# An accumulating DMA in place of a subtraction, in the two stages that have tokens on the partitions

## The chip, the core and the metric

The kernel runs on one core of one Trainium2 chip. The time is device time of one execution, in microseconds. The kernel before takes 2176.35 us (median of two runs, 2176.28 and 2176.42).

A core has five engines with a queue of instructions each: TensorE (PE in the profile; PEld is its load of weights), VectorE (DVE), ScalarE (ACT), GpSimd (POOL) and SyncE (SP). Sixteen DMA engines move data between memory and the on-chip buffer, or inside that buffer. SP issues the loads here; they go out on a hardware queue. A DMA that POOL issues goes out on a software queue.

## What is computed

Two transformer blocks, one after the other, on 256 tokens of 2048 features, all in float32:

```
x = x + attention(rms_norm(x)) @ w_o                      # stick-breaking attention, 16 heads
x = x + relu(rms_norm(x) @ w1)**2 @ w2                    # 8192 hidden features
x = rms_norm(x)
m = concat(attention(z), pooling(z)) @ w_o_2              # z = rms_norm(x) @ w_in, 8 heads
x = x + rms_norm(m, post_mix_g)
up = causal_dwconv(rms_norm(x) @ w_up)                    # 2 x 5632 features
y = (gelu(up[:, :5632]) * up[:, 5632:]) @ w_down
x = x + rms_norm(y, post_ffn_g)
```

The two products behind which a norm of its own follows (`@ w_o_2` and `@ w_down`) are the two stages of the change.

## The kernel before

**Operands in two parts.** Every large product takes its operands in two parts: hi, the 12 leading bits (type float32r), and lo, the rest. Three of the four partial products are formed: hi x hi, hi x lo and lo x hi. The weights come from memory in float32 and are split on the chip.

**Units.** The weights are cut into about 400 units of at most 1024 KB (128 partitions x 2048 values). A unit is loaded into a tile raw (three of these), split into hi and lo by halves of 1024 columns (six tiles of each, so three units' worth), and multiplied. For each half, ScalarE writes hi (line 159: a copy of raw that rounds) and VectorE then writes lo = raw - hi (line 160).

**The order** is written out by hand at the end of `tile_two_blocks`. While unit i is multiplied, the load of unit i + 3 is issued on SP and the two halves of unit i + 2 are split; the part of a split that follows on another engine is emitted one place later (`rest`). Engines serve their instructions in the order in which they stand, each with its waits: a load waits until the raw tile's last reader is done, a split until PE is done with the unit whose hi and lo tiles it takes over.

**The two stages.** In most products the features are on the partitions. In the output projection of the second block (`w_o2`, 16 units of four blocks of K) and in the four passes over `w_down` (12 units each: 4 result chunks x units of 4, 4 and 3 blocks) the tokens are: hi and lo of the weights stream through PE as the moving operand (lines 218 to 220). Each w_down pass follows a fourth of the gated features (`w_up`, 22 units), whose last results, `ff`, it reads: POOL multiplies gate and value (line 908), ScalarE and VectorE split the result (lines 126 and 129).

Of the kernel before, what the change touches and what calls it, by code (L numbers as in the profile page):

```python
# [8 lines left out]
F32 = mybir.dt.float32  # L9
# [22 lines left out]

# Features are on the partitions and tokens along a row, but for the values of
# the attentions and for the two sums behind which a norm of its own follows:
# there the tokens are on the partitions.
#
# Every large product takes its operands in two parts, the 12 leading bits
# (float32r, exact in one pass) and the rest; three of the four partial
# products carry float32's accuracy.


class Unit:
    """One stretch of weights: its load, its split in two parts, its products."""

    def __init__(self, src, blocks, width, mm, evac):
        self.src = src
        self.blocks = blocks
        self.width = width
        self.mm = mm
        self.evac = evac  # L50
        self.acc = None
        self.halves = []

# [9 lines left out]
def tile_two_blocks(ctx: ExitStack, tc: tile.TileContext, xT, w_q_k, w_v, w_o, w1, w2,  # L63
# [48 lines left out]
    def later(n, fn):  # L112
        """Emit it n places on, when the other engines have what it needs."""
        if st.get("now"):
            fn()
        else:
            queue.setdefault(clock[0] + n, []).append(fn)

    def hold(first, n, step=None, place="A"):
        """The results of n units stay in PSUM until this step."""  # L120
        for k in range(first, first + n):
            late[k] = (first + n if step is None else step, place)

# [1 line left out]
    def hi_copy(dst, src, scale=1.0):  # L125
# [28 lines left out]
    def split(i, eng=V):  # L154
        """Two pieces of work, and what follows each of them a place later."""
        raw = units[i].raw
        for a, b, hi, lo in halves(i):
            hi, lo = hi[:, 0:b - a], lo[:, 0:b - a]
            A.activation(out=hi, in_=raw[:, a:b], func=AF.Copy)
            yield lambda a=a, b=b, hi=hi, lo=lo: eng.tensor_tensor(  # L160
                out=lo, in0=raw[:, a:b], in1=hi.bitcast(F32), op=ALU.subtract)

# [1 line left out]
    def block(u, j, op, first, last):  # L164
        """out[:, 0:T] + out[:, T:] gathers the three partial products."""
        hi, lo = u.w(j)
        if last:
            PE.matmul(u.acc[:, 0:T], lhsT=lo, rhs=op[:, 0:T], start=False, stop=False)  # L168
            PE.matmul(u.acc, lhsT=hi, rhs=op, start=False, stop=True)  # L169
        else:  # L170
            PE.matmul(u.acc, lhsT=hi, rhs=op, start=first, stop=False)  # L171
            PE.matmul(u.acc[:, 0:T], lhsT=lo, rhs=op[:, 0:T], start=False, stop=False)  # L172

    def features(u, ops, order=None, part=None):
        """Products with the features on the partitions: all of K, or a part of its order."""
        order = range(u.blocks) if order is None else order
        a, b = part or (0, len(order))
        if a == 0:
            u.acc = accum("acc")
        for n in range(a, b):  # L180
            block(u, order[n], ops[order[n]], n == 0, n == len(order) - 1)

    def pair(i, ops, order, tail, mid=None, end=None):
        """Two units at once: both take the operands that come last at the end."""
        u, v = units[i], units[i + 1]
        n = len(order)
        features(u, ops, order, (0, n - tail))
        if mid:
            mid()
        features(v, ops, order, (0, n - tail))  # L190
        features(u, ops, order, (n - tail, n))
        features(v, ops, order, (n - tail, n))
        if end:
            end()

    def keep_warm(n):
        """Products that nothing reads, where the tensor engine waits: its clock would halve."""
        ps = aux("ps_warm")
        for _ in range(n):
            PE.matmul(ps[:, 0:P], lhsT=ones, rhs=ones, start=True, stop=True)  # L200
# [4 lines left out]
    def tokens(some, accs, first, last, one_by_one):  # L205
        """Products with the tokens on the partitions, for a part of K."""
        wide = [slice(0, 512)]
        todo = [(n, k, t, c) for n, (u, _) in enumerate(some) for k in range(u.blocks)
                for t in range(2) for c in (HALVES if len(accs) > 2 and t else wide)]
        if one_by_one:  # L210
            todo.sort(key=lambda x: (x[2], x[3].start))
        for n, k, t, c in todo:
            u, ops = some[n]
            hi, lo = u.w(k)
            xh = ops[k][:, t * P:(t + 1) * P]
            xl = ops[k][:, T + t * P:T + (t + 1) * P]
            acc = accs[2][:, c] if c.start else accs[t][:, c]
            PE.matmul(acc, lhsT=xh, rhs=hi[:, c], start=first and n == k == 0, stop=False)  # L218
            PE.matmul(acc, lhsT=xh, rhs=lo[:, c], start=False, stop=False)  # L219
            PE.matmul(acc, lhsT=xl, rhs=hi[:, c], start=False,  # L220
                      stop=last and n == len(some) - 1 and k == u.blocks - 1)

    def token_units(srcs, ops, evac, apart=0):
        """The units of 512 result features: srcs has (weights, their tiles of K) of each.
        The last units (their number is apart) do one half of the tokens before the other."""
        accs = []
# [7 lines left out]
        for j, (src, nk) in enumerate(srcs):  # L234
# [9 lines left out]
            def ev(u, j=j):  # L244
                if j == n - 1:
                    evac(accs)
            units.append(Unit(src, nk, 512, mm, ev))
            at_k += nk

    def whole(u):  # L250
        """The second of the two sums, on its way to be added."""
        t = t256("half")
        A.activation(out=t, in_=u.acc[:, T:2 * T], func=AF.Copy)  # L253
        return t

# [1 line left out]
    class Stat:  # L257
# [21 lines left out]
    def root(src, dst):  # L279
        """(src / D + eps) ** -0.5, of a column or two."""  # L280
        n = src.shape[-1]
# [24 lines left out]

    # ================= the units =================
    xin = []
# [4 lines left out]

    # -- first block: q and k of each head, then v
    qk = {}
# [50 lines left out]
    def later_only(ap, fill):  # L366
        """A value where the key is not before the query: in the two diagonal blocks."""
        d = ap[:, 0:384].rearrange("p (b q) -> p b q", b=3)[:, 0:3:2, :]
# [85 lines left out]

    # -- output projection: the residual, and what feeds the MLP
    a2 = {}
# [40 lines left out]

    # -- MLP, a fourth of the hidden features at a time
    hid = {}
# [20 lines left out]
    def pairs(first, ops, n, tail, mid=None, end=None):  # L520
        """What the units of a new set of operands do: the first two go together."""
        def f(m):
# [20 lines left out]

    # -- second block
    B2 = len(units)
# [11 lines left out]

    # the residual turns its tokens onto the partitions
    resT = {}
# [85 lines left out]

    # -- pooling over trailing windows
    BU = len(units)
# [48 lines left out]

    # -- v, with the map of the pooled features between its chunks
    BV2 = len(units)
# [28 lines left out]
    class Ordered:  # L727
        """The operands of the output projection: first those that are there first."""
        def __getitem__(self, k):
            return o2[(k + 8) % 16]  # L730

    # -- output projection, with tokens on the partitions: a norm follows
    mg = {}
# [48 lines left out]
    for n in range(NC):  # L782
        token_units([(w_o2[n, j], 4) for j in range(4)], Ordered(), evac_o2(n), 1 if n == NC - 1 else 0)

    # -- gated feed-forward, a fourth of its features at a time
    BF = len(units)
# [178 lines left out]
    for fc in range(FC):  # L965
# [12 lines left out]
        for n in range(NC):  # L978
            w = w_down[fc, n]
            token_units([(w[:, a * 512:min(a + 4, FT) * 512], min(4, FT - a)) for a in range(0, FT, 4)],  # L980
                        ff, evac_down(fc, n), 2 if fc == FC - 1 and n == NC - 1 else 0)
    for n in range(4):
        hold(BF + n, 1, BF + 3 + n % 2, "C")

    # ================= the program =================
    gains = {}
# [101 lines left out]
def _blocks(w, kt, nt):  # L1088
    """(K, N) -> (N tiles, 128, K tiles, 128), each of them in one piece."""
    return w.reshape(kt, P, nt, P).transpose(2, 1, 0, 3)  # L1090


def _rows(w, kt, nc):
    """(K, N) -> (chunks of 512, fourths of K, 128, K tiles, 512)."""
    return w.reshape(4, kt // 4, P, nc, 512).transpose(3, 0, 2, 1, 4)
# [59 lines left out]
```

## Time and profile before

| | |
|---|---|
| median of the runs | 2176.35 us (2176.28 to 2176.42) |
| profiled execution, its span | 2174.6 us |
| PE busy | 2156.1 us, 99% |
| DVE, ACT, POOL busy | 1433.2, 1112.3, 201.3 us |
| moved by DMA | 401.13 MB, 184 GB/s over the span |

No time of its own is shown for the profiled execution but its span, from the first to the last instruction; it is 1.75 us under the median of the runs. Busy time says how much an engine did, not whether anyone waited for it: that is read from the chain of waits, and from the windows of the single stages. PE's ends are modelled, so 99% busy is not PE at its peak.

### The profile page before, as it was taken

To read this page: it belongs to the slowest core of one execution; us is meant where nothing else is said; L and a number is where in the kernel's file an instruction comes from. 1 tells how busy PE (TensorE), PEld (TensorE's weight loads), DVE (VectorE), ACT (ScalarE), POOL (GpSimd) and SP (SyncE) were. 2 spreads that over 40 slices of the span, in tenths; PEclk is the share of its full clock that TensorE was granted. 3 is DMA by queue.
4 is the path that set the end of the run, shared out by engine and by line. 5 is a ranking of instruction groups with operands and counts; after the bars stand their busy time and mean duration, and the time that the engine had idled before them with its cause. 6 is when DMAs were issued, how large, how long until landed. Compare 5 with 4: busy or idle time off the path is not lost.

```text
span 2174.6 us, 29627 instructions
## 1 busy us (share of the span) xinstructions
PE 2156.1 (99%) x11765; PEld 1858.6 (85%) x11765; DVE 1433.2 (66%) x2038; ACT 1112.3 (51%) x1682; POOL 201.3 (9%) x281
## 2 busy tenths in 40 slices
PE   8999999999999999999999999999999999999997
PEld 7888888888888888888888888888888888888886
DVE  8776546665565556556656665488758857866885
ACT  5555445454354355345546544466546545544653
POOL 4000001000000000000120150011101101100110
PEclk9999999999999999999999999999999999999999
DMA  7454545555555555555555555545555565555553
GB/s 256 157 173 173 177 162 187 176 192 194 177 192 192 178 190 178 191 186 182 194 175 193 179 184 192 203 143 186 202 194 184 180 200 192 178 190 194 189 204 111
DMA packets 60106, 401.13 MB, mean 184 GB/s; under 512 B 6848, under 2 KB 8000, under 8 KB 14144
## 3 DMA queue, kind: packets, MB, share of 16 engines
q1 hardware_dynamic: 59184, 397.13, 53.1%
q0 software_dynamic: 640, 2.10, 0.3%
q8 instruction: 93, 1.52, 0.3%
q14 instruction: 45, 0.37, 0.0%
q10 hardware_dynamic: 144, 0.01, 0.0%
HBM read 397.11 MB, written 2.10 MB: 184 GB/s over the span
## 4 chain that ended last, share of the span: by engine, by line
PE 98%; DVE 1%; issue 0%; ACT 0%; POOL 0%; DMA 0%; DVEq 0%; POOLq 0%
PE acc L171 46%; PE acc L172 23%; PE acc L218 7%; PE acc L220 7%; PE acc L219 7%; PE acc L169 3%; PE acc L168 2%; PE ps_o L436 0%; PE ps_z L362 0%; DVE xin L132 0%; DVE y L960 0%; PE ps_o L437 0%; PE ps_back L801 0%; PE ps_z L363 0%; PE ps_s L406 0%
## 5 line engine op out<-in xcount | busy, mean ns | idle before, releaser
L253 ACT ACTIVATE half<-acc 128x256 f32<-128x256 f32 x208 | 77.7, 377 | 215.9 <-PE acc L169 213.8
L462 DVE TENSOR_TENSOR res<-acc,res 128x256 f32<-128x256 f32 x80 | 33.9, 424 | 136.4 <-PE acc L169 136.4
L268 POOL TENSOR_TENSOR s<-s,sq 128x256 f32<-128x256 f32 x45 | 32.7, 741 | 861.1 <-ACT sq L267 861.1
L893 POOL TENSOR_TENSOR s<-s,c 128x256 f32<-128x256 f32 x44 | 36.1, 822 | 449.3 <-DVE s L892 449.3
L874 ACT ACTIVATE c<-half,vec 128x256 f32<-128x256 f32 x88 | 52.3, 595 | 35.6 <-DVE half L870 35.6
L511 ACT ACTIVATE sq_relu<-half 128x256 f32<-128x256 f32 x64 | 26.8, 419 | 71.3 <-DVE half L507 71.3
L881 DVE SCALAR_TENSOR_TENSOR c<-half,vec,c 128x254 f32<-128x254 f32 x88 | 58.0, 659 | 3.1
L897 ACT ACTIVATE s<-s 128x256 f32<-128x256 f32 x44 | 18.3, 418 | 71.0 <-POOL s L893 71.0
L126 ACT ACTIVATE ff<-c 128x256 fp32r<-128x256 f32 x44 | 18.4, 418 | 70.0 <-POOL c L908 69.9
L870 DVE TENSOR_TENSOR half<-half,rb 128x256 f32<-128x256 f32 x88 | 50.9, 578 | 3.1
L908 POOL TENSOR_TENSOR c<-gate,c 128x256 f32<-128x256 f32 x44 | 36.4, 827 | 146.1 <-DVE gate L902 138.7
L879 DVE SCALAR_TENSOR_TENSOR c<-half,vec,c 128x255 f32<-128x255 f32 x88 | 42.4, 482 | 0.0
L869 DVE TENSOR_TENSOR half<-acc,half 128x256 f32<-128x256 f32 x88 | 36.8, 418 | 0.0
L463 DVE TENSOR_TENSOR res<-acc,res 128x256 f32<-128x256 f32 x80 | 34.0, 425 | 2.7
L126 ACT ACTIVATE o<-ps_o 128x256 fp32r<-128x256 f32 x24 | 9.2, 384 | 50.9 <-PE ps_o L437 50.9
L506 DVE TENSOR_TENSOR half<-acc,half 128x256 f32<-128x256 f32 x64 | 26.8, 418 | 4.9 <-ACT half L253 4.9
L129 DVE TENSOR_TENSOR hid<-sq_relu,hid 128x256 fp32r<-128x256 f32 x64 | 26.8, 419 | 3.7 <-ACT hid L126 3.7
L507 DVE SCALAR_TENSOR_TENSOR half<-half,rb 128x256 f32<-128x256 f32 x64 | 27.2, 426 | 2.2
L126 ACT ACTIVATE a<-res,vec 128x256 fp32r<-128x256 f32 x16 | 8.1, 509 | 40.1 <-DVE res L463 40.1
L126 ACT ACTIVATE hid<-sq_relu 128x256 fp32r<-128x256 f32 x64 | 26.9, 420 | 2.0
L938 DVE TENSOR_TENSOR y<-acc,y 128x512 f32<-128x512 f32 x23 | 15.8, 692 | 16.8 <-PE acc L220 16.8
L392 ACT ACTIVATE sp_hi<-e 128x384 fp32r<-128x384 f32 x16 | 8.3, 524 | 35.5 <-POOL e L369 35.5
(6172 smaller groups left out, 8290.8 us busy)
## 6 DMA issues: line engine op xcount, KB each, us to landing
raw<-in_w SPq DMA_DIRECT2D x128, 1024.0 KB, 4.8
raw<-in_w_up SPq DMA_DIRECT2D x88, 1024.0 KB, 4.7
raw<-in_w_q_k SPq DMA_DIRECT2D x45, 1024.0 KB, 4.8
raw<-in_w_o SPq DMA_DIRECT2D x32, 1024.0 KB, 4.8
raw<-in_w_down SPq DMA_DIRECT2D x32, 1024.0 KB, 4.8
raw<-in_w_v SPq DMA_DIRECT2D x24, 1024.0 KB, 4.7
raw<-in_w_down SPq DMA_DIRECT2D x16, 768.0 KB, 4.1
raw<-in_w_u SPq DMA_DIRECT2D x8, 1024.0 KB, 4.8
```

The lines of the kernel that those rows point to most:

```text
L126: A.activation(out=dst[:, 0:T], in_=src, func=AF.Copy, scale=scale)
L168: PE.matmul(u.acc[:, 0:T], lhsT=lo, rhs=op[:, 0:T], start=False, stop=False)
L169: PE.matmul(u.acc, lhsT=hi, rhs=op, start=False, stop=True)
L171: PE.matmul(u.acc, lhsT=hi, rhs=op, start=first, stop=False)
L172: PE.matmul(u.acc[:, 0:T], lhsT=lo, rhs=op[:, 0:T], start=False, stop=False)
L218: PE.matmul(acc, lhsT=xh, rhs=hi[:, c], start=first and n == k == 0, stop=False)
L219: PE.matmul(acc, lhsT=xh, rhs=lo[:, c], start=False, stop=False)
L220: PE.matmul(acc, lhsT=xl, rhs=hi[:, c], start=False, stop=last and n == len(some) - 1 and k == u.blocks - 1)
L253: A.activation(out=t, in_=u.acc[:, T:2 * T], func=AF.Copy)
L870: V.tensor_tensor(out=t, in0=t, in1=st["rb6"], op=ALU.mult)
L874: A.activation(out=c, in_=t, func=AF.Identity, bias=cw[:, 4 * n + 3:4 * n + 4], scale=cw[:, 4 * n + 2:4 * n + 3])
L881: V.scalar_tensor_tensor(out=c[:, 2:T], in0=t[:, 0:T - 2], scalar=cw[:, 4 * n:4 * n + 1], in1=c[:, 2:T], op0=ALU.mult, op1=ALU.add)
```

## The change

A unit has a new field, `rest`. It is set for the units of the output projection ("chip") and of w_down ("memory"), and for no others. In such a unit a half is split in another way. ScalarE writes hi as before. ScalarE then writes -hi into lo, as a second copy of raw with the scale -1. A DMA that POOL issues adds the float32 weights onto lo: from the raw tile on the chip ("chip"), or a second time from the weights in memory ("memory"). The subtraction of VectorE falls away.

```diff
@@ class Unit
         self.acc = None
+        self.rest = None
         self.halves = []
@@ def split(i, eng=V)
-        raw = units[i].raw
+        raw, kind = units[i].raw, units[i].rest
         for a, b, hi, lo in halves(i):
             hi, lo = hi[:, 0:b - a], lo[:, 0:b - a]
             A.activation(out=hi, in_=raw[:, a:b], func=AF.Copy)
-            yield lambda a=a, b=b, hi=hi, lo=lo: eng.tensor_tensor(
-                out=lo, in0=raw[:, a:b], in1=hi.bitcast(F32), op=ALU.subtract)
+            if kind:
+                A.activation(out=lo, in_=raw[:, a:b], func=AF.Copy, scale=-1.0)
+                src = raw[:, a:b] if kind == "chip" else units[i].src[:, a:b]
+                yield lambda lo=lo, src=src: G.dma_start(out=lo, in_=src, accum_op=ALU.add)
+            else:
+                yield lambda a=a, b=b, hi=hi, lo=lo: eng.tensor_tensor(
+                    out=lo, in0=raw[:, a:b], in1=hi.bitcast(F32), op=ALU.subtract)
@@ def token_units
-    def token_units(srcs, ops, evac, apart=0):
+    def token_units(srcs, ops, evac, apart=0, rest=None):
...
             units.append(Unit(src, nk, 512, mm, ev))
+            units[-1].rest = rest
@@ the output projection
-        token_units([(w_o2[n, j], 4) for j in range(4)], Ordered(), evac_o2(n), 1 if n == NC - 1 else 0)
+        token_units([(w_o2[n, j], 4) for j in range(4)], Ordered(), evac_o2(n), 1 if n == NC - 1 else 0, "chip")
@@ w_down
-                        ff, evac_down(fc, n), 2 if fc == FC - 1 and n == NC - 1 else 0)
+                        ff, evac_down(fc, n), 2 if fc == FC - 1 and n == NC - 1 else 0, "memory")
```

The rest of the diff takes comments out. Lines move down by one at first and by seven behind `token_units`: line 159 becomes 160, 893 becomes 900.

Over the whole program VectorE loses 128 instructions, ScalarE gains 128 and POOL gains 128; PE and SP keep theirs.

ScalarE in the output projection, before (hi of two units; the words in brackets are the semaphores that a row waits for: DMAHW a hardware queue, DMASW the software queue):

```order
L159 ACTIVATE hi__12075<-raw_12035 128x1024 [waits DMAHW0_49,DVE_49,PE_49]
L159 ACTIVATE hi__12079<-raw_12035 128x1024 [waits DVE_49,PE_49]
L159 ACTIVATE hi__12109<-raw_12073 128x1024 [waits DMAHW1_49,DVE_49,PE_49]
L159 ACTIVATE hi__12113<-raw_12073 128x1024 [waits DVE_49,PE_49]
L744 ACTIVATE junk,c_12141<-acc 128x512 [waits PE_49] x2
```

The same two units after:

```order
L160 ACTIVATE hi__12083<-raw_12041 128x1024 [waits DMAHW0_49,PE_49,Activation_49]
L162 ACTIVATE lo__12084<-raw_12041 128x1024 [waits DMASW2_49]
L160 ACTIVATE hi__12088<-raw_12041 128x1024 [waits PE_49,Activation_49]
L162 ACTIVATE lo__12089<-raw_12041 128x1024 [waits DMASW3_49]
L160 ACTIVATE hi__12119<-raw_12081 128x1024 [waits DMAHW1_49,PE_49,Activation_49]
L162 ACTIVATE lo__12120<-raw_12081 128x1024 [waits DMASW0_49]
L160 ACTIVATE hi__12124<-raw_12081 128x1024 [waits PE_49,Activation_49]
L162 ACTIVATE lo__12125<-raw_12081 128x1024 [waits DMASW1_49]
L751 ACTIVATE junk,c_12153<-acc 128x512 [waits PE_49] x2
```

Four copies of 128x1024 became eight, all ahead of the sums of squares of the last result chunk.

POOL at the start of the first w_down pass, after (before, the rows of lines 893 and 908 that answer to 900 and 915 here follow one another with nothing between them):

```order
L900 TENSOR_TENSOR s<-s,c 128x256 [waits DVE_49,Activation_49,Pool_49]
L915 TENSOR_TENSOR c<-gate,c 128x256 [waits DVE_49,Activation_49]
L164 DMA lo__13939<-in_w_down 128x1024 [waits PE_49,Activation_49]
L164 DMA lo__13948<-in_w_down 128x1024 [waits DMASW7_49,PE_49,Activation_49]
L900 TENSOR_TENSOR s<-s,c 128x256 [waits DVE_49,Pool_49]
L164 DMA lo__13997<-in_w_down 128x1024 [waits DMASW1_49,DMASW6_49,PE_49,Activation_49]
L915 TENSOR_TENSOR c<-gate,c 128x256 [waits DVE_49]
L164 DMA lo__14007<-in_w_down 128x1024 [waits PE_49,Activation_49]
L164 DMA lo__14056<-in_w_down 128x1024 [waits DMASW0_49,PE_49,Activation_49]
L164 DMA lo__14065<-in_w_down 128x512 [waits PE_49,Activation_49]
L900 TENSOR_TENSOR s<-s,c 128x256 [waits DVE_49,Pool_49]
L164 DMA lo__14104<-in_w_down 128x1024 [waits DMASW4_49,PE_49,Activation_49]
```

The last gated features now stand on POOL behind issues of accumulates, and each issue waits for a copy on ScalarE.

SP at the loads of the output projection, after (before, each of these waits for VectorE's subtraction and the earlier load):

```order
L140 DMA raw_12041<-in_w_o 128x2048 [waits DMASW3_49,DMAHW5_49,DMASW2_49,Activation_49]
L140 DMA raw_12081<-in_w_o 128x2048 [waits DMASW1_49,DMAHW6_49,DMASW0_49,Activation_49]
L140 DMA raw_12117<-in_w_o 128x2048 [waits DMASW3_49,DMAHW7_49,DMASW2_49,Activation_49]
L140 DMA raw_12162<-in_w_o 128x2048 [waits DMASW5_49,DMAHW0_49,DMASW4_49,Activation_49]
L140 DMA raw_12200<-in_w_o 128x2048 [waits DMASW7_49,DMAHW1_49,DMASW6_49,Activation_49]
```

A load in this stage now waits until both accumulates have read the raw tile that it takes over.

## Rows read from the trace of the kernel before

**Rows 1.** Page, busy us (share of the span) and instructions of each engine.

```profile
PE 2156.1 (99%) x11765; PEld 1858.6 (85%) x11765; DVE 1433.2 (66%) x2038; ACT 1112.3 (51%) x1682; POOL 201.3 (9%) x281
```

**Rows 2.** Page, PE in 40 slices, and the chain that ended last.

```profile
PE   8999999999999999999999999999999999999997
...
PE 98%; DVE 1%; issue 0%; ACT 0%; POOL 0%; DMA 0%; DVEq 0%; POOLq 0%
PE acc L171 46%; PE acc L172 23%; PE acc L218 7%; PE acc L220 7%; PE acc L219 7%; PE acc L169 3%; PE acc L168 2%; PE ps_o L436 0%; PE ps_z L362 0%; DVE xin L132 0%; DVE y L960 0%; PE ps_o L437 0%; PE ps_back L801 0%; PE ps_z L363 0%; PE ps_s L406 0%
```

**Rows 3.** Windows of the output projection and the four w_down passes.

```profile
core 0: us, PE busy (x) PEld busy (x) DVE busy (x) ACT busy (x) POOL busy (x), PEclk, DMA share, GB/s
1328.80:1419.20 90.40, 90.40 (x449) 76.95 (x448) 45.66 (x47) 40.48 (x54) 0.57 (x1) 1.00 0.56 192
1550.30:1610.10 59.80, 59.80 (x265) 49.54 (x264) 33.18 (x38) 29.50 (x38) 3.14 (x3) 1.00 0.59 200
1734.50:1794.30 59.80, 59.80 (x265) 49.55 (x264) 35.37 (x42) 26.36 (x30) 2.41 (x2) 1.00 0.60 200
1918.70:1978.50 59.80, 59.80 (x265) 49.56 (x264) 35.36 (x42) 26.36 (x30) 2.41 (x2) 1.00 0.59 200
2102.90:2164.40 61.50, 60.49 (x298) 51.21 (x296) 38.57 (x51) 26.40 (x40) 6.02 (x6) 1.00 0.43 150
```

**Rows 4.** The same windows, the subtraction (L160) alone.

```profile
1328.80:1419.20 90.40, 38.51 (x32) 0.00 (x0) 1.00 0.56 192
...
sum 331.30, DVE 143.16 POOL 0.00; mean DVE 28.63 POOL 0.00
```

**Rows 5.** The same windows, ScalarE's copy (L159) alone.

```profile
1328.80:1419.20 90.40, 33.33 (x32) 1.00 0.56 192
1550.30:1610.10 59.80, 23.10 (x24) 1.00 0.59 200
```

**Rows 6.** DMA in 1328.8 to 1419.2, in 1550.3 to 1610.1, and slices of 1335 to 1345.

```profile
q1 hardware_dynamic: 2370, 17.32, 55.8%
...
raw<-in_w_o SPq DMA_DIRECT2D x11, 1024.0 KB, 4.8
...
q1 hardware_dynamic: 1744, 11.93, 58.3%
...
DMA  7999999910000000000000000000020099214999
GB/s 328 459 393 459 459 426 393 393 66 0 0 0 0 0 0 0 0 0 0 0 0 0 0 0 0 0 0 0 0 66 0 0 328 197 33 33 197 459 459 459
```

**Rows 7.** Timeline of ScalarE; in brackets the idle time before, and who ended it.

```profile
1358.82 1.06 ACT L159 ACTIVATE hi__12192<-raw 128x1024 fp32r<-128x1024 f32 x1 [1.66 <-PE acc L220]
```

**Rows 8.** The gains' software queue: issues on POOL, then DMA in 1304 to 1311.

```profile
L739 POOL DMA_DIRECT2D gain<-in_g_post x8: 536/546/759, 1304.7 to 2103.3; - x8
...
q0 software_dynamic: 320, 1.05, 42.3%
q1 hardware_dynamic: 137, 0.99, 36.3%
...
gain<-in_g_post POOLq DMA_DIRECT2D x8, 256.0 KB, 4.0
```

**Rows 9.** Timeline at the start of the first w_down pass: POOL, ACT, DVE, PE.

```profile
1560.80 1.58 POOL L908 TENSOR_TENSOR c<-gate,c 128x256 f32<-128x256 f32 x1 [3.14 <-DVE gate L902]
...
1562.42 0.42 ACT L126 ACTIVATE ff<-c 128x256 fp32r<-128x256 f32 x1 [2.41 <-POOL c L908]
...
1562.87 0.43 DVE L129 TENSOR_TENSOR ff<-c,ff 128x256 fp32r<-128x256 f32 x1 [1.08 <-ACT ff L126]
...
1563.88 0.39 PE L218 MATMUL acc<-hi__14027,ff 128*128 128x512 f32 x1
```

## The prediction

> **What bounds the kernel now.** I read the busy table first [rows 1]: TensorE is busy 2156.1 of 2174.6 us, so at most 18.5 us of the whole span is not matrix work. The chain that ended last [rows 2] says the same from the other side: 98% of it is PE, and nearly all of that is the lines of the products. VectorE, the engine that the change relieves, holds 1% of the chain, and the subtraction of line 160 is not among the lines listed.
>
> Then I cut the span into the stages that the change touches [rows 3]: the output projection of the second block (1328.8 to 1419.2 us, 16 units) and the four passes over w_down (12 units each). In the first four of these five windows PE is busy for all of the window, with the clock at 1.00, which is the 2.4 GHz level. What the reader should see there is the DMA share, 0.56 to 0.60: the sixteen DMA engines are the second busiest resource, with 40% free. VectorE is busy for 51 to 59% of those four windows (45.66 of 90.40, 35.37 of 59.80), most of it in the subtraction [rows 4].
>
> Sizes per unit. An output-projection unit takes PE 90.4 / 16 = 5.65 us. A w_down pass moves 8 units of 1024 KB and 4 of 768 KB, 11 full units' worth, so 59.8 / 11 = 5.44 us each. For a load, queue 1 used 55.8% of 90.4 us for 17.32 MB [rows 6]: 50.4 us of all sixteen engines for 16.5 pieces of 1024 KB (1.049 MB), or **3.06 us per 1024 KB**. The w_down window gives the same (58.3% of 59.8 us for 11.93 MB).
>
> **What the change removes.** Per half unit, one VectorE subtraction: 128 in all by the order lists, and 143 us over the five windows [rows 4]. It is worth nothing in time: no PE wait in these windows ends on it, since PE is never idle in the first four of them.
>
> **What it adds on ScalarE.** One more copy of the same shape per half. Over the stages ScalarE now spends 23 to 33 us on its copies [rows 5]; doubling them brings it from 40.5 to 74 of 90.4 us, and from 29.5 to 53 of 59.8. It still fits: a copy now waits 1.66 us for PE to give a buffer back [rows 7], and the new one fills that gap. I cost it at nothing in steady state; if ScalarE ran late, PE would wait for what is over a unit's time, and it is 10% short of that.
>
> **What it adds on POOL.** Two DMA issues per unit, 0.55 us each by the one software-queue issue there is [rows 8]; POOL is busy 0.57 to 3.14 us in the first four windows. POOL serves in order, though, and each issue waits for its negated copy. At the start of each w_down pass this stands between the last hidden features: now the last two products on POOL end at 1562.38, ScalarE's copy at 1562.84, VectorE's rest at 1563.30, and PE reaches the last of those blocks at 1563.88 [rows 9]. So the slack is 0.6 us. One or two extra copies ahead of it (1.05 us each) make 0.5 to 2 us of stall; about 2 us in four passes is **8 us**, if PE isn't already late there for another reason.
>
> **What it adds on the DMA engines.** This is the term that decides. Each unit's 1024 KB passes them a second time, and not as a copy: the old contents of lo must be fetched too, added, and written back. The trace has no accumulating transfer, so I bound its cost r per 1024 KB.
>
> Low end: it costs what a copy costs. The software queue's four 256 KB loads took 42.3% of a 7 us window for 1.05 MB, 2.96 us of sixteen engines [rows 8], so that queue is as good as the hardware one: r = 3.06. Lower still: the load bursts reach 459 GB/s in single slices [rows 6], 2.3 us per 1024 KB.
>
> High end: three movements (two reads and a write that don't overlap), r = 9.2; four would be 12.2. I take **two movements, r = 6.1**: a copy's row already covers one read with its write, and the accumulate adds exactly one more read of the same size through the same engines. The upper values need a loss that no row hints at.
>
> On this the Trainium skill has a price, which no run here shows: "Collectives: The Full Stack", Part 3, "Why ReduceScatter is half of AllGather", holds that the add itself is free and that both source reads go through one ring, 62.28 against 32.35 GB/s measured. By its ratio of 1.93, r would be an estimated 5.9 us and the added time about 12 us less than by my two movements.
>
> **The sum.** The first accumulate of a stage can be issued two units ahead of it, when its buffers come free; the last must land by the start of the last unit. What the DMA engines must do in that stretch beyond what PE needs is the delay.
> - Output projection: PE 17 x 5.65 = 96 us. DMA 16 x 6.1 + 17 loads x 3.06 = 150. Delay 54.
> - A w_down pass followed by w_up: PE 2 x 5.65 + 59.8 - 4.1 (the last unit) = 67. DMA 11 x 6.1 + 12 x 3.06 = 104. Delay 37, three times 110.
> - The last pass has nothing to load for a next stage: 67.1 + 10 x 3.06 = 98, delay 31.
>
> Together 195 us. The 8 us of the pass starts are inside it, as PE waits there for lo anyway. 2174.6 + 195 = 2370. The medians shown are 1.75 us above this profiled span, so **2371 us**. Nothing gives this back: w_up stages are bound by PE, and their unit (PE 5.65 us, load 3.06) refills only three units' buffers.
>
> **Rivals.**
> - *Not slower: the transfers hide.* If r is 2.4 us or less (the burst rate, with both reads overlapped), a unit needs 3.06 + 2.4 = 5.46 us of DMA against 5.44 of PE, and nothing shows but the pass starts, 0 to 8 us: 2176 to 2185. At a copy's r = 3.06 the same sums give 5 + 3 x 3.4 + 0 = 15, and with the 8 about 2199. Both are within 2%. That line (43.5 us) is crossed at r = 3.4, as every us of r is 16 + 44 = 60 us of time. For the hiding: the busy share of a DMA engine may hold waiting that two queues overlap. Against it: one load alone fills its slices to 9 tenths while it runs [rows 6].
> - *Three movements or worse.* r = 9.2: 103 + 3 x 71 + 65 = 381, so 2557; r = 12.2: 2737. What would speak for it is a read-modify-write that can't be pipelined row by row.
> - *The transfers follow one another.* A load of 1024 KB lands 4.8 us after its issue, one of 256 KB on the software queue 4.0 [rows 6, 8]. If a unit's two halves ran strictly one behind the other at 4.8 us, a unit would take 9.6 us: (9.6 - 5.65) x 16 + (9.6 - 5.44) x 44 = 246, less two units' lead in each of five stages (about 11 each), some 190. That lands beside my forecast for another cause; the DMA share would stay near 0.6.
> - *Late by latency alone.* Copy 1.05, copy 1.05, issue 0.55, landing 4.8 are 7.5 us; a half's buffers come free two and a half units, some 14 us, ahead of its use. So this costs nothing unless landing doubles.
> - *A gain.* Faster by 2% needs 43.5 us; PE leaves 18.5 in all, and by the slices of [rows 2] most of it lies in the first and the last of the forty, outside the stages' products. That the change doesn't do what it says is out: the order lists show 128 subtractions gone, 128 copies and 128 accumulates come.
>
> **Numbers.** Forecast, two movements or one behind the other (2290 to 2440): 0.45. Hidden or nearly (below 2220): 0.19. Between (2220 to 2290, r of 3.4 to 4.7): 0.10. Above 2440: 0.25, half of it over 2620. Gain: 0.01. A range of **2190 to 2620** leaves out the gain and the fully hidden case (0.08) and the worst (0.12). 2% is about what a measurement of this kernel is read by; faster 0.01, within 0.19, slower 0.80.
>
> **What would show it.** In the windows of the stages the DMA share goes from 0.56 to 0.9 or more, PE's busy share falls to about 62%, and PE waits for the accumulate; a w_down pass takes about 96 us in place of 59.8, the w_up stretches keep theirs. A software queue of 3 us per 1024 KB with PE still full would prove me wrong, as would PE waiting for ScalarE or for POOL with the DMA engines half idle. If the share stays near 0.6 and PE waits for the accumulate all the same, the third rival holds.

## Result, and the profile after

The changed kernel takes **2310.48 us** (two runs, 2310.39 to 2310.58) against 2176.35: 134.1 us more, a ratio of 1.0616 (95% interval 1.0596 to 1.0637). It is slower, as forecast, by two thirds of the 195 us.

The page of the profile: busy table, slices of PE and DMA, queues, and the chain that ended last.

```profile
PE 2197.5 (95%) x11765; PEld 1866.8 (81%) x11765; DVE 1296.2 (56%) x1910; ACT 1222.9 (53%) x1810; POOL 309.3 (13%) x409
...
PE   8999999999999999999999988998899899979986
...
DMA  7445545555555555555555599558955985796598
...
q1 hardware_dynamic: 59184, 397.13, 49.4%
q0 software_dynamic: 19072, 65.02, 14.3%
...
PE 78%; DMA 15%; issue 3%; ACT 1%; POOL 1%; DVE 1%; POOLq 0%; SPq 0%; DVEq 0%; ACTq 0%
```

Where [rows 2] had 98% PE, the chain now has 15% DMA. VectorE lost 137 us of work, and nobody got them: the subtraction is in no line of the chain of [rows 2]. The DMA slices rise to 9 at five places, and at the same five PE falls. Those are the stages.

The same stages by windows (columns as in [rows 3]: length, busy time of PE, PEld, DVE, ACT and POOL, clock, DMA share, GB/s). Below them are the stretch from the projection to the first pass and a w_up stretch between two passes, each after and then before:

```profile
1328.80:1455.00 126.20, 102.22 (x448) 81.70 (x447) 9.76 (x14) 64.58 (x81) 25.82 (x32) 0.92 1.03 263
1589.40:1674.40 85.00, 66.25 (x265) 47.83 (x264) 10.29 (x14) 47.90 (x60) 21.35 (x25) 1.00 1.03 274
1798.80:1882.70 83.90, 68.82 (x265) 51.65 (x264) 14.86 (x21) 44.03 (x52) 20.48 (x24) 0.94 1.03 274
2007.10:2091.80 84.70, 67.25 (x266) 50.83 (x265) 14.92 (x21) 44.06 (x52) 19.92 (x23) 0.96 1.02 272
2216.10:2298.70 82.60, 66.02 (x298) 51.73 (x296) 17.34 (x30) 43.89 (x62) 24.86 (x29) 0.96 0.96 245
...
1455.00:1589.40 134.40, 131.89 (x759) 115.14 (x758) 112.19 (x187) 86.24 (x154) 24.48 (x28) 0.99 0.53 180
1419.20:1550.30 131.10, 130.50 (x759) 113.70 (x758) 111.86 (x184) 83.83 (x150) 22.18 (x24) 1.00 0.49 170
...
1674.50:1798.80 124.30, 124.30 (x705) 107.83 (x704) 97.10 (x151) 75.84 (x120) 17.59 (x23) 1.00 0.57 188
1610.10:1734.50 124.40, 124.40 (x706) 107.90 (x705) 101.00 (x155) 73.24 (x118) 15.56 (x20) 1.00 0.53 183
```

The DMA share is 1.02 to 1.03 in place of 0.56 to 0.60, and 0.96 in place of 0.43 in the last pass: by the time of their packets the sixteen engines are full. A share above 1 means that packets overlap in time on an engine. ScalarE and POOL are far from full. From the start of the projection to that of the first pass it is 39.1 us more than before, 35.8 of them in the projection itself. From the start of one pass to that of the next it is 25.2, 24.1 and 24.8 us more, and from the start of the last pass to the end of the program 20.9. That is 134.1. The w_up stretches keep their 124.3 to 124.4 us.

PE's clock falls in some of these windows, but it does not set their length: the first pass has 1.00 and takes 85.0 us, the second has 0.94 and takes 83.9.

Waits of PE, the five longest that fall in these stages (who waited, for whom, us in total, times, longest):

```profile
PE acc L225 <- DMA lo__19073<-in_w_down: 5.0, 1, 5.0
PE acc L225 <- DMA lo__12165<-raw: 3.7, 1, 3.7
PE acc L225 <- DMA lo__12319<-raw: 3.5, 1, 3.5
PE acc L225 <- DMA lo__12393<-raw: 3.5, 1, 3.5
PE acc L225 <- DMA lo__12239<-raw: 2.7, 1, 2.7
```

Line 225 is the product with lo. What PE waits for is the accumulate, not a load or a copy.

What one accumulate costs is read from the two queues in the projection's window (33.24 MB in 126.2 us), in the part of it from 1345 to 1440 us, and in the first pass's window (23.31 MB in 85.0 us): packets, MB, share.

```profile
q0 software_dynamic: 4544, 16.39, 66.2%
q1 hardware_dynamic: 2294, 16.79, 36.7%
...
q0 software_dynamic: 3424, 12.45, 68.6%
...
q0 software_dynamic: 3308, 11.00, 65.7%
q1 hardware_dynamic: 1801, 12.26, 37.5%
```

For 1024 KB (1.049 MB), the accumulate from memory takes 0.657 x 85.0 / 11.00 x 1.049 = **5.32 us**. The projection's window also holds four plain loads of the gains on the software queue (1.05 MB); behind them, in 1345 to 1440, the accumulate from the chip takes 0.686 x 95 / 12.45 x 1.049 = **5.49 us**. A load costs 2.89 us in the projection and 2.73 in the pass, where it cost 3.06 alone [rows 6].

### The profile page after: what moved, and what is told of

The parts are those of the page before. It is cut to its first block, busy times and chain, and to the rows that moved or that the text cites. A ratio compares the mean times of both kernels' runs of the same rounds, so it can differ in the third digit from the quotient of the medians.

```text
span 2308.7 us, 29886 instructions
## 1 busy us (share of the span) xinstructions
PE 2197.5 (95%) x11765; PEld 1866.8 (81%) x11765; DVE 1296.2 (56%) x1910; ACT 1222.9 (53%) x1810; POOL 309.3 (13%) x409
## 4 chain that ended last, share of the span: by engine, by line
PE 78%; DMA 15%; issue 3%; ACT 1%; POOL 1%; DVE 1%; POOLq 0%; SPq 0%; DVEq 0%; ACTq 0%
PE acc L177 41%; PE acc L178 21%; PE acc L225 3%; PE acc L226 3%; PE acc L175 3%; PE acc L224 3%; DMA raw<-in_w_o 2%; PE acc L174 1%; DMA lo__19281<-in_w_down 1%; DMA lo__17488<-in_w_down 1%; DMA lo__15787<-in_w_down 1%; DMA lo__19073<-in_w_down 1%; DMA lo__16033<-in_w_down 1%; DMA lo__17563<-in_w_down 1%; DMA lo__17700<-in_w_down 1%
## 5 line engine op out<-in xcount | busy, mean ns | idle before, releaser
L886 DVE SCALAR_TENSOR_TENSOR c<-half,vec,c 128x255 f32<-128x255 f32 x88 | 51.0, 579 | 13.6 <-ACT c L881 13.3
L130 DVE TENSOR_TENSOR ff<-c,ff 128x256 fp32r<-128x256 f32 x44 | 18.2, 415 | 28.0 <-ACT ff L127 28.0
```

Of the source, the lines that this page charges most:

```text
L130: V.tensor_tensor(out=dst[:, T:2 * T], in0=src, in1=dst[:, 0:T].bitcast(F32), op=ALU.subtract)
L886: V.scalar_tensor_tensor(out=c[:, 1:T], in0=t[:, 0:T - 1], scalar=cw[:, 4 * n + 1:4 * n + 2], in1=c[:, 1:T], op0=ALU.mult, op1=ALU.add)
```

## The experiments

Each ran beside the kernel before on the same chip. The theory: in the two stages the sixteen DMA engines are the bound, because an accumulate costs them 1.7 times a copy. The rivals: whatever POOL issues is late; the longer queue of ScalarE; the source; the rows of a transfer; the software queue's own pace.

**A copy in place of the accumulate.**

```diff
-                yield lambda lo=lo, src=src: G.dma_start(out=lo, in_=src, accum_op=ALU.add)
+                yield lambda lo=lo, src=src: G.dma_start(out=lo, in_=src)
```

> Everything as in the changed kernel, but the DMA of POOL copies the weights over lo and adds nothing; the rest of the weights is left out of lo. Theory (the DMA engines are full, and an accumulate costs them 5.3 us per 1024 KB where a copy costs about 3, since it also fetches the old contents): the software queue's share of a w_down window falls to a cost of 2.7 to 3.1 us per 1024 KB, a unit needs some 5.8 us of DMA against 5.44 to 5.65 of PE, and the time is 2180 to 2200 us. Rival (any transfer that POOL issues is late, whatever it does with the bytes): still 2290 to 2310 us, with PE waiting for lo as much as now.

Measured: 2204.9 us, ratio 1.0127 [1.0109, 1.0144], 5 us above the theory's span and 106 below the changed kernel. The first pass by windows and queues, then the projection by windows and its software queue in 1345 to 1410:

```profile
1563.90:1629.10 65.20, 61.94 (x265) 50.53 (x264) 9.96 (x14) 47.33 (x60) 13.90 (x25) 0.97 1.00 353
...
q1 hardware_dynamic: 1795, 12.23, 51.8%
q0 software_dynamic: 3240, 10.72, 48.1%
...
1328.80:1432.90 104.10, 93.29 (x449) 77.97 (x448) 11.79 (x19) 64.85 (x81) 17.00 (x33) 0.98 0.94 324
...
q0 software_dynamic: 2762, 10.07, 42.8%
```

From memory the copy costs 0.481 x 65.2 / 10.72 x 1.049 = 3.07 us per 1024 KB, as the prediction's low end had it, and the accumulate is 1.73 times that. From the chip it costs 0.428 x 65 / 10.07 x 1.049 = 2.90, and the accumulate is 1.89 times that. Same bytes, same issues, same order: 28 us are due to a second passage of the bytes at all, 106 us to the accumulating. In the first pass even the copies fill the engines (share 1.00), at 353 GB/s against 274. In the projection they don't (0.94), and yet it takes 104.1 us in place of 90.4, with PE waiting for lo: half of the 28 us is lost where they are not quite full, and what it is there stays open. The rival falls.

**ScalarE's second copy, and no DMA.** VectorE adds the weights onto the negated copy.

```diff
-                yield lambda lo=lo, src=src: G.dma_start(out=lo, in_=src, accum_op=ALU.add)
+                yield lambda a=a, b=b, lo=lo: eng.tensor_tensor(
+                    out=lo, in0=raw[:, a:b], in1=lo.bitcast(F32), op=ALU.add)
```

> ScalarE still writes the negated copy into lo, but VectorE adds the weights onto it; no DMA of POOL. Theory (the loss is the DMA engines' alone, and ScalarE's 128 copies fit beside PE): 2176 to 2180 us. Rival (ScalarE's longer queue makes the last gated features late at the pass starts, or delays the splits): 2184 us or more, with PE waiting at the pass starts for ff.

Measured: 2179.72 us, ratio 1.0015 [1.0005, 1.0025]. The rest of the loss is the DMA's. The 2 to 3 us lie where the rival put them: the first w_down pass takes 62.2 us in place of 59.8, and PE waits there for the last gated features (who waited, for whom, then VectorE's timeline):

```profile
PE acc L225 <- ACT ff L127: 1.5, 1, 1.5
PE acc L227 <- DVE ff L130: 0.2, 1, 0.2
...
1563.19 1.23 DVE L164 TENSOR_TENSOR lo__14104<-raw,lo__14104 128x1024 fp32r<-128x1024 f32 x1 [2.10 <-ACT lo__14104 L162]
1564.34 0.42 DVE L910 SCALAR_TENSOR_TENSOR gate<-s,c 128x256 f32<-128x256 f32 x1
```

VectorE's addition waits 2.10 us for ScalarE's second copy, and the gate, from which POOL makes the last product, stands behind it. The later passes lose 0.3 us each. So the pass starts are worth 3 us in all here, not the 8 of the prediction. In the changed kernel they are covered, as it said: there PE is late for lo by then.

**Nothing adds the weights.** Neither a DMA of POOL nor VectorE.

```diff
-                yield lambda lo=lo, src=src: G.dma_start(out=lo, in_=src, accum_op=ALU.add)
+                yield lambda: None
```

> ScalarE writes hi and the negated copy, and nothing adds the weights: no DMA of POOL, no VectorE; lo is left at -hi. Theory (VectorE's subtraction covered nothing that PE waited for): 2176 to 2181 us, no faster than the kernel before, and within 3 us of the kernel in which VectorE adds. Rival (VectorE's relief is worth something that the accumulate's cost hid): 2172 us or less.

Measured: 2176.16 us, ratio 0.9998 [0.9989, 1.0008]. The 143 us that VectorE spends on the subtraction [rows 4] are worth nothing. The time is 3.6 us under that of the kernel in which VectorE adds, where I had allowed 3. ScalarE makes all of its second copies here too, so they cost nothing by themselves: the 3 us of the run before need VectorE's addition behind them.

**Half of the accumulates.** The second half of each unit is subtracted on VectorE.

```diff
-            if kind:
+            if kind and a == 0:
```

> The accumulate is used for the first half of each unit of the two stages only; the second half is subtracted on VectorE as before. Theory (throughput: 3.06 us of load and 2.7 of accumulate per unit, overlapped by some 3%, come to 5.5 us, about PE's 5.44 to 5.65): nearly all of the 134 us comes back, 2178 to 2195 us. Rival (latency: each accumulate lands too late by itself): half of the loss stays, some 2240 us, with the DMA share well under 1.

Measured: 2196.47 us, ratio 1.0092 [1.0077, 1.0108], just over the theory's span. Half of the accumulates cost 20 us, all of them 134: not the same price for each, but more like a resource that overflows. By windows of the projection and the first pass:

```profile
1328.80:1422.60 93.80, 91.16 (x449) 76.65 (x449) 29.50 (x33) 52.57 (x68) 12.85 (x16) 1.00 0.99 278
1553.60:1618.30 64.70, 61.37 (x265) 49.21 (x264) 22.10 (x25) 38.76 (x49) 11.54 (x14) 1.00 0.99 282
```

The engines are just full (0.99). The rival, lateness of each transfer by itself, wanted a share well under 1. The prediction's sum, with the rates measured above, gives no loss here: 8 x 5.49 + 17 x 2.89 = 93 us against PE's 96 in the projection, 6 x 5.32 + 12 x 2.73 = 65 against 67 in a pass. The projection is 3.4 us longer all the same, and the first pass 4.9: near the line the sum is short.

**Sources exchanged.**

```diff
-        token_units([(w_o2[n, j], 4) for j in range(4)], Ordered(), evac_o2(n), 1 if n == NC - 1 else 0, "chip")
+        token_units([(w_o2[n, j], 4) for j in range(4)], Ordered(), evac_o2(n), 1 if n == NC - 1 else 0, "memory")
...
-                        ff, evac_down(fc, n), 2 if fc == FC - 1 and n == NC - 1 else 0, "memory")
+                        ff, evac_down(fc, n), 2 if fc == FC - 1 and n == NC - 1 else 0, "chip")
```

> The sources are exchanged: the output projection adds from memory, w_down adds from the raw tile on the chip. Theory (what counts is the time on the DMA engines, 5.3 us per 1024 KB from either source): 2300 to 2320 us, the windows of both stages as long as now. Rival A (the second read of memory competes with the loads): w_down passes get shorter, 75 us or less in place of 85, and the time 2265 to 2280. Rival B (a raw tile held until the accumulate has read it delays the loads): w_down passes get longer, 90 us or more, and the time over 2325.

Measured: 2322.5 us, ratio 1.0668 [1.0652, 1.0684], between theory and rival B. The projection takes 1 to 2 us more than in the changed kernel, the first three passes 90.9, 87.4 and 83.8 in place of 85.0, 83.9 and 84.7 us. Rival A falls: memory is not what is short. Of rival B there is a trace. SP's loads in the first pass now wait for the accumulate that still reads their raw tile, and the share there is 0.96 (below, behind the window, the software queue in the projection from 1345 to 1440 us and in the first pass):

```profile
SPq L140 <- DMA lo__14112<-raw: 11.5, 1, 11.5
SPq L140 <- DMA lo__14007<-raw: 10.4, 1, 10.4
...
1588.30:1679.20 90.90, 70.45 (x265) 54.40 (x264) 10.10 (x14) 47.04 (x60) 21.39 (x25) 0.89 0.96 244
...
q0 software_dynamic: 3650, 13.26, 70.3%
...
q0 software_dynamic: 3176, 10.49, 61.2%
```

The engines spend as much time in this window as in the changed kernel's (0.96 x 90.9 = 87 us, 1.03 x 85.0 = 88), so the 6 us are not more work for them. PE's clock is 0.89 there too: how much is the held tile and how much the slower PE stays open. The price follows the source by a few per cent: 0.703 x 95 / 13.26 x 1.049 = 5.28 us from memory, now in the projection, and 0.612 x 90.9 / 10.49 x 1.049 = 5.56 from the chip.

**Rows of 8 KB, with a control.** The control lays both halves of lo in one tile:

```diff
+        u.lo = wp.tile([P, 2048], F32R, tag="lo", name=f"lo{i}_", bufs=3)
...
-            lo = wp.tile([P, 1024], F32R, tag="lo", name=f"lo{i}_", bufs=6)
+            lo = u.lo[:, a * u.width:b * u.width]
```

> A control for the next kernel: the two halves of lo lie in one tile of 2048 columns (three of these in place of six halves); still two accumulates of 4 KB rows per unit. Both theories below: within 15 us of the changed kernel, 2300 to 2325 us; a first half's buffer may come free half a unit later.

Measured: 2310.45 us, ratio 1.0615 [1.0599, 1.0631]: the tile's form costs nothing. Then one accumulate per unit, issued with the second half:

```diff
+                n = units[i].blocks * units[i].width
+                src = raw[:, 0:n] if kind == "chip" else units[i].src[:, 0:n]
+                lo = units[i].lo[:, 0:n]
+                yield (lambda lo=lo, src=src: G.dma_start(out=lo, in_=src, accum_op=ALU.add)) if a else (lambda: None)
```

> As the kernel with the joint tile, but one accumulate per unit, with rows of 8 KB (6 KB in the units of three blocks). Theory (an accumulate costs the DMA engines by its bytes, about 1.75 times a copy): the software queue's cost stays 5.0 to 5.5 us per 1024 KB, and the time 2300 to 2340 us, somewhat later for the first half of each unit. Rival (it costs by its rows, 128 per transfer, whatever their length): 2.7 us per 1024 KB, and 2185 to 2215 us.

Measured: 2328.82 us, ratio 1.0700 [1.0684, 1.0716].

**Rows of 2 KB.**

```diff
+                def short(lo=lo, src=src):
+                    m = lo.shape[-1] // 2
+                    for s in (slice(0, m), slice(m, 2 * m)):
+                        G.dma_start(out=lo[:, s], in_=src[:, s], accum_op=ALU.add)
+                yield short
```

> As the changed kernel, but each accumulate in two transfers of half the columns, with rows of 2 KB. Theory (cost by bytes): 5.3 to 6.0 us per 1024 KB, 2310 to 2350 us. Rival (cost by rows): 10.6 us per 1024 KB, over 2550 us. Twice the issues on POOL, 0.87 us each, come to 3.5 us per unit, which fits in either case.

Measured: 2325.44 us, ratio 1.0679 [1.0662, 1.0697]. The software queue over the whole program, with rows of 8 and of 2 KB (4 KB is the changed kernel, shown above):

```profile
q0 software_dynamic: 9856, 65.02, 13.7%
```

```profile
q0 software_dynamic: 37504, 65.03, 15.6%
```

Less some 6 us for the gains' loads and over 60 pieces of 1024 KB: 5.2 us (0.137 x 2326.2 = 319), 5.4 (0.143 x 2308.7 = 330) and 5.9 (0.156 x 2326.1 = 363). The cost follows the bytes; the rival's 2.7 and 10.6 are far off. Longer rows save 4% of the accumulate's time, and yet that kernel is 18 us slower than its control. The first half of a unit now waits for the second, and single waits of PE grow to 6.9 us:

```profile
PE acc L228 <- DMA lo__11756<-raw: 6.9, 1, 6.9
```

In its first pass the DMA share is 0.99 and the clock 0.89; how the 18 us split between longer waits and lower clock is not shown.

**Smaller loads.** In w_down only 1024 columns of a unit are loaded, and ScalarE makes both halves from them; the accumulates stay whole.

```diff
+        n = n if u.rest != "memory" else min(n, 1024)
-        nc.sync.dma_start(out=u.raw[:, 0:n], in_=u.src)
+        nc.sync.dma_start(out=u.raw[:, 0:n], in_=u.src[:, 0:n])
...
+            part = raw[:, 0:b - a] if kind == "memory" else raw[:, a:b]
...
```

> As the changed kernel, but each unit of w_down loads its first 1024 columns only, and ScalarE makes both halves of hi and of the negated copy from them; the accumulates still read all of the weights from memory. So hi and -hi of a second half hold other weights. Theory (loads and accumulates share the same sixteen engines, which are full): 11 accumulates of 5.4 us and loads of half the size come to about 77 us per pass and its two units ahead, where PE needs 67, so a w_down pass of 68 to 73 us in place of 85, and 2255 to 2270 us in all. Rival (the software queue alone sets the pace, whatever the loads do): passes stay at 83 to 86 us, and the time at 2305 to 2315.

Measured: 2273.83 us, ratio 1.0447 [1.0432, 1.0463], 4 us above the theory's span; the first three passes take 76.2, 75.2 and 73.9 us. The rival falls: accumulates that are untouched get done sooner when loads are taken away. My figure for the pass, 68 to 73, was 1 to 3 us short; that the loads saved ahead of a pass save nothing would explain it, but is not shown. The first pass:

```profile
1589.80:1666.00 76.20, 65.67 (x265) 47.93 (x264) 10.29 (x14) 47.78 (x60) 21.58 (x25) 1.00 1.04 260
...
q0 software_dynamic: 3303, 10.97, 73.3%
q1 hardware_dynamic: 1795, 8.78, 30.2%
```

The window moved 8.78 MB of loads in place of 12.26, 3.3 pieces less; at 2.73 us each that is 9.1 us, and the pass is 8.8 us shorter. The engines are still full, and an accumulate costs what it did: 0.733 x 76.2 / 10.97 x 1.049 = 5.34 us.

**The projection alone.** w_down goes back to VectorE.

```diff
-                        ff, evac_down(fc, n), 2 if fc == FC - 1 and n == NC - 1 else 0, "memory")
+                        ff, evac_down(fc, n), 2 if fc == FC - 1 and n == NC - 1 else 0)
```

> Only the output projection takes the accumulate; w_down subtracts on VectorE as before. Theory (each stage pays its own DMA time, and nothing is carried over): the projection's 36 us and the 3 us behind it in the changed kernel's trace, 2213 to 2218 us, all other stretches as in the kernel before. Rival (the stages pay for each other, for instance by loads that stay late): under 2205 or over 2225 us.

Measured: 2215.19 us, ratio 1.0178 [1.0163, 1.0194], as the theory had it. The stages don't pay for each other. The projection takes the same 126.2 us as in the changed kernel, with the clock at 0.95 in place of 0.92: here too the clock does not set the length.

No variant beats the kernel before, and this route has little to win: PE is busy for 99% of the span there, and what VectorE gives up nobody needs.

## Why the prediction was right, and where its size was off

**The bound, the cover and the sign held.** VectorE's subtraction was worth nothing (0.9998 without it). The accumulate overfilled the DMA engines, PE waited for lo, the w_up stretches kept their time. The share went to 0.96 to 1.03 (forecast 0.9 or more), PE's busy share to 78 to 82% of the windows (forecast 62%), a pass to 85 us (forecast 96).

**The term that was mis-sized is r.** I took 6.1 us per 1024 KB, two movements; measured are 5.49 from the chip and 5.32 from memory, or 1.89 and 1.73 plain copies from the same source. The second term is the load: 3.06 us alone, 2.89 and 2.73 beside accumulates. With these four rates in the sum as it stands:
- projection 16 x 5.49 + 17 x 2.89 - 96 = 41.0 (measured 35.8, with the stretch behind it 39.1);
- a pass 11 x 5.32 + 12 x 2.73 - 67 = 24.3 (25.2, 24.1, 24.8);
- the last 11 x 5.32 + 10 x 2.73 - 67 = 18.8 (20.9).

Together 133 us, measured 134. So the accounting holds where the engines are overfull, and its price for the accumulate was about a seventh too high. The rates come from the same windows, so the sum tests the counts and the leads more than the rates; that the rate is steady is shown by the run with smaller loads (5.34). Since only the excess over PE's time is paid, 10 to 13% on r and 6 to 11% on the load became a third of the forecast loss.

The Trainium skill's price, from "Collectives: The Full Stack", Part 3, "Why ReduceScatter is half of AllGather", was a ratio of 1.93. The measured 1.73 and 1.89 lie nearer to it than to my 2, and by the page's ratio the added time would have been an estimated 183 us, still too much. Whether the part above one copy is the second read, as the page has it, or the adding, no run here tells apart: that stays open.

**The rivals.** The hidden case failed at once: a plain copy costs 2.90 to 3.07 us, not 2.4, and even that shows as 28 us (my sum for it gave 23, of which 5 in the projection, where 13.7 were measured). Three movements did not come. Transfers one behind the other would have kept the share near 0.6. Lateness by latency as the main cause is out by the run with half of the accumulates and by the one with smaller loads.

**One slip.** I let the first accumulate of a pass start two units, 11 us, ahead. It started 7 us ahead, and the last gated product of the first pass stood behind seven accumulates on POOL (timeline of POOL and PE; in brackets the idle time before, and who ended it):

```profile
1582.41 0.90 POOL L164 DMA_DIRECT2D lo__13939<-in_w_down  x1 [3.40 <-ACT s L896]
1584.62 0.88 POOL L164 DMA_DIRECT2D lo__13948<-in_w_down  x1 [1.30 <-ACT lo__13948 L162]
1585.19 1.06 POOL L900 TENSOR_TENSOR s<-s,c 128x256 f32<-128x256 f32 x1
...
1599.86 0.89 POOL L164 DMA_DIRECT2D lo__14104<-in_w_down  x1 [2.64 <-ACT lo__14104 L162]
1600.48 1.05 POOL L915 TENSOR_TENSOR c<-gate,c 128x256 f32<-128x256 f32 x1
...
1589.39 0.40 PE L224 MATMUL acc<-hi__13938,ff 128*128 128x512 f32 x1
1606.15 0.39 PE L224 MATMUL acc<-hi__14055,ff 128*128 128x512 f32 x1
```

That product ends at 1601.53, and PE, late itself, opens the unit that reads it at 1606.15: the order on POOL cost nothing here, where [rows 9] had 0.6 us to spare. The shorter lead alone would add 4 us to the sum. The sum also lacked the 0.03 above a share of 1, worth about 2.5 us in a pass, which works the other way; no run takes the two apart.

## What to carry to other kernels

Before work is moved from a compute engine to the DMA engines, price it in their time, stage by stage: share already used, plus bytes times the cost per byte of that kind of transfer, against the time of the engine that sets the pace. Far below that line it should cost nothing; at the line it already costs some (half of the accumulates: 20 us), above it every microsecond is paid, and an error of a tenth in the price becomes a third of the loss. An engine that is busy for 60% of a stage but in no chain has nothing to give; one at 56% that feeds the bound has less room than it seems.

## What the runs showed of the hardware

- An accumulating DMA took 5.3 us of all sixteen engines per 1024 KB from memory and 5.5 from the chip, where a plain one took 3.07 and 2.90.
- The rows of an accumulate hardly matter: 5.9, 5.4 and 5.2 us per 1024 KB at 2, 4 and 8 KB.
- The profile's row for the issue of an accumulate lasts 0.86 to 0.90 us in the pass, for a plain copy of the same shape 0.54 to 0.60. But POOL's next instruction starts 0.57 and 0.62 us behind the issue in the rows above (1584.62, 1599.86), so the row is longer than POOL is held. Nor is it the accumulating alone: the gains' plain loads, 0.55 before [rows 8] and 0.56 among copies, have a median of 0.88 in the changed kernel:

```profile
L746 POOL DMA_DIRECT2D gain<-in_g_post x8: 546/876/907, 1328.0 to 2219.6; - x8
```

- The waits of PE cost clock as well. Behind the projection, with PE idle for half of the 5 us before, the mean clock was 0.69, between the two levels of 1.2 and 2.4 GHz. The stretch from the projection to the first pass is 3.3 us longer than before, by the windows 1.9 us of it more idle time of PE and 1.4 more busy time:

```profile
1455.00:1460.00 5.00, 2.56 (x22) 2.15 (x20) 4.38 (x11) 0.49 (x3) 1.57 (x2) 0.97 1.00 398
1460.00:1465.00 5.00, 4.93 (x25) 4.72 (x26) 3.69 (x9) 3.46 (x7) 0.82 (x1) 0.69 0.07 25
```
